# Low halves of one stage's weights prepared a stage earlier, and a rotation moved from GpSimd to VectorE

## The chip, the cores and the metric

The kernel runs on 1 core of one Trainium2 chip. The metric is the device time of one execution in microseconds; lower is better. Engines are named as in the profile: PE (TensorE), PEld (its weight loads), DVE (VectorE), ACT (ScalarE), POOL (GpSimd) and SP (SyncE, which issues nearly all DMAs).

## What is computed

Two blocks of two layers each on a 256 x 1024 float32 activation. The part that matters here:

```python
x = sandwich(x, mod, g_pre, g_post, ffn)          # stages 1 and 3: SwiGLU, D_FF = 2816
...
def fox_s5_mixer(x, ...):                          # stage 4
    q, k, v, f_logit, u = split(x @ w_in)
    att = forgetting_attention(q, k, v, f_logit + f_bias)
    y = s5_scan(u, ...)                            # h_t = a h_(t-1) + b u_t, complex a
    y = gelu(y); y = y * sigmoid(y @ w_glu + b_glu)
    return concatenate([att, y]) @ w_out
```

The complex recurrence of `s5_scan` is computed in a frame that turns with the angle of `a`: the input is turned in with tables of cosines and sines, a real scan with the magnitude of `a` runs on the real and the imaginary part, and the result is turned out with the same tables.

## The kernel before

The network runs as eight stages in a row (`run`, L2234 on): hybrid mixer, FFN, dilated attention, FFN (stage 3), attention with state space (stage 4, `even`), mixture of experts, mLSTM, mixture of experts.

**Weights.** Every projection weight is cut into units of 128 x 1024 float32 (512 KB, counted as 0.524 MB here). A product is made of three float32r matmuls: high weight times high activation, low times high, high times low. So each unit needs a high half `whi` (the weight rounded to float32r) and a low half `wlo` (what the rounding left out). `raw` (L287) lets SP load a unit into one of six buffers `raw`; `prepare` (L317) then casts it on ACT into `whi` (L328) and subtracts on DVE into `wlo` (L329). For the first three units of a stage and those of two named weights the subtraction is POOL's (L325). `whi` and `wlo` have five buffers each; during an FFN its output weights use three more. `split` (L332) hands out the next unit in the fixed order of `plan_of` (L343) and keeps two more prepared ahead, also across the stage boundary: the last units of stage 3 prepare the first three of stage 4.

**Background work.** Each unit handed out counts one tick; every `EVERY[st]` ticks (L690) one step of a background generator runs (`tick`, `step`). In stage 3 the generator is `modulation(3)`: eight steps, each a 512 KB load and one DVE pass of 128 x 1024 (L719). `drain` runs what is left. Instructions inside `later()` are placed behind the last evacuations of the stage join on their engine.

**Stage 3** (`ffn`, L760 on) takes 66 units: four at the start, then 21 times two input units and one output unit, less the ends. Between them ACT and DVE make the hidden values (`fs` L768, `fh` L770, `fhh`, `fhl`), on which the next output product waits.

**Stage 4** (`even`, L1522 on) has 26 units: 4 `ev_u`, 4 `ev_v`, 8 `ev_qk`, 8 `ev_out`, 2 `s5_glu`. Its attention (`fox`) and its state space (`state_space`) alternate. `state_space(jj)` runs four times with four quarters each. A quarter: PE projects into `eb` (L1576); DVE turns in with two products from PSUM (L1580, L1581), an add and a subtract within SBUF (L1582, L1583), and two scans (L1587); POOL turns out with two products of 128 x 512 (`eoc` L1590, `eos` L1591). After four quarters PE sums them into `ey` (L1597) and DVE adds the skip term (L1599). The order of instructions on each engine, SP's queue included, is fixed when the program is built; each engine and queue works through its own in order and waits on semaphores.

Of the kernel before, what the change touches and what calls it, by code (L numbers as in the profile page):

```python
# [9 lines left out]
F32 = mybir.dt.float32  # L10
F32R = mybir.dt.float32r
# [4 lines left out]
ALU = mybir.AluOpType  # L16
# [11 lines left out]
UNIT = 1024  # L28
# [199 lines left out]
class K:  # L228
# [87 lines left out]
    def prepare(self):  # L316
        nc = self.nc  # L317
        name, i = self.plan.pop(0)
        r = self.raw(name, i)
        pool = self.xtra.get(name, self.spl)  # L320
        hi = pool.tile([128, UNIT], F32R, tag="whi", name=self.nm("whi"))
        lo = pool.tile([128, UNIT], F32R, tag="wlo", name=self.nm("wlo"))
        if (name, i) in self.early:
            nc.scalar.copy(hi, r)  # L324
            nc.gpsimd.tensor_tensor(lo, r, hi.bitcast(F32), op=ALU.subtract)  # L325
        else:
            with self.later():
                nc.scalar.copy(hi, r)  # L328
                nc.vector.tensor_tensor(lo, r, hi.bitcast(F32), op=ALU.subtract)  # L329
        self.ready.append(((name, i), hi, lo))  # L330

    def split(self, name, i):  # L332

# [353 lines left out]
                self.feat(act, t, x, None, None)  # L687
        return act

    EVERY = (0.9, 1.6, 1.5, 2.0)  # L690


    def mod_setup(self):
# [65 lines left out]
    def ffn(self, act, l, hook=None):  # L759
        nc = self.nc  # L760
        ps = [[self.pso("fo") for n in range(2)] for t in range(2)]
        with self.tc.tile_pool(name=f"ff{l}", bufs=2) as P, self.tc.tile_pool(name=f"fx{l}", bufs=3) as X:

            def hidden(p):
                hh = P.tile([128, 256], F32R, tag="fhh", name=self.nm("fhh"), bufs=self.HOLD + 1)
                hl = P.tile([128, 256], F32R, tag="fhl", name=self.nm("fhl"), bufs=self.HOLD + 1)
                s = P.tile([128, 256], F32, tag="fs", name=self.nm("fs"))
                nc.scalar.activation(s, p[:, 0:256], AF.Silu)  # L768
                h = P.tile([128, 256], F32, tag="fh", name=self.nm("fh"))
                nc.vector.tensor_tensor(h, s, p[:, 256:512], op=ALU.mult)  # L770
                self.split_act(hh, hl, h)
                return hh, hl

            self.xtra = {"ffn_out": X}

            pp = [self.psw("pt"), self.psw("pt")]
            self.proj_b(act, "ffn_in", l * 44, 4, pp, True)
            if hook is not None:
                with self.later():
                    hook(P)  # L780
            hs = [[P.tile([128, 256], F32R, tag=g, name=self.nm(g), bufs=self.HOLD + 1) for g in ("fhh", "fhl")]
                  for j in range(2)]
            for t in range(2):
                ts = slice(t * 128, t * 128 + 128)
                s = P.tile([128, 256], F32, tag="fs", name=self.nm("fs"))
                nc.scalar.activation(s, pp[t][:, 0:256], AF.Silu)
                h = P.tile([128, 256], F32, tag="fh", name=self.nm("fh"))
                nc.vector.tensor_tensor(h, s, pp[t][:, 256:512], op=ALU.mult)
                pt = self.psw("fT")
                for j in range(2):  # L790
                    o = pt[:, j * 128:j * 128 + 128]
                    nc.tensor.transpose(o, h[:, j * 128:j * 128 + 128], self.ident)
                    self.split_act(hs[j][0][:, ts], hs[j][1][:, ts], o)
            late = []
            for j in range(22):
                if 2 <= j:
                    hs.append(None)
                    p = self.proj_a2(act, "ffn_in", l * 44 + j * 2)
                    self.down(ps, hs[j - 1], "ffn_out", l * 22 + j - 1, False, False, late if j > 22 - self.HOLD else None)
                    hs[j] = hidden(p)  # L800
                elif j == 0:
                    self.down(ps, hs[0], "ffn_out", l * 22, True, False)
            self.down(ps, hs[21], "ffn_out", l * 22 + 21, False, True, late)
            self.run_late(late)
            self.xtra = {}
        return ps

# [713 lines left out]
    def even(self, act):  # L1521
        nc, tc, a = self.nc, self.tc, self.a  # L1522
        with tc.tile_pool(name="ev", bufs=1) as P:
# [36 lines left out]
            def state_space(jj):  # L1560

                bt = self.rawp.tile([128, 4, 2, 128], F32, tag="raw", name=self.nm("raw"))
                nc.sync.dma_start(out=bt.rearrange("p a b c -> p (a b c)"), in_=a["s5_b"][jj])
                tabs = []
                for i in range(2):
                    tb = self.rawp.tile([128, 2, 2, 256], F32, tag="raw", name=self.nm("raw"))
                    nc.sync.dma_start(out=tb.rearrange("p a b c -> p (a b c)"), in_=self.s5d[jj * 2 + i])
                    tabs.append(tb)
                outs = []
                for q in range(4):  # L1570
                    j = jj * 4 + q
                    cb = tabs[q // 2][:, q % 2, 0:1, :].to_broadcast([128, 2, 256])
                    sb = tabs[q // 2][:, q % 2, 1:2, :].to_broadcast([128, 2, 256])
                    pb = self.psw("eb")
                    for i in range(2):
                        nc.tensor.matmul(pb[:, i * 256:(i + 1) * 256], bt[:, q, i, :], uT[:, jj, :], start=True, stop=True)  # L1576
                    pbv = pb.rearrange("p (i t) -> p i t", i=2)
                    m = self.tmp.tile([128, 2, 2, 256], F32, tag="big", name=self.nm("em"), bufs=2)
                    m1, m2 = m[:, 0], m[:, 1]
                    nc.vector.tensor_tensor(m1, pbv, cb, op=ALU.mult)  # L1580
                    nc.vector.tensor_tensor(m2, pbv, sb, op=ALU.mult)  # L1581
                    nc.vector.tensor_tensor(m1[:, 0], m1[:, 0], m2[:, 1], op=ALU.add)  # L1582
                    nc.vector.tensor_tensor(m1[:, 1], m1[:, 1], m2[:, 0], op=ALU.subtract)  # L1583
                    h = P.tile([128, 2, 256], F32, tag="eh", name=self.nm("eh"), bufs=2)
                    mg = self.s5m[:, j:j + 1].to_broadcast([128, 256])
                    for i in range(2):
                        nc.vector.tensor_tensor_scan(h[:, i, :], mg, m1[:, i, :], 0.0, ALU.mult, ALU.add)  # L1587
                    oc = P.tile([128, 2, 256], F32, tag="eoc", name=self.nm("eoc"), bufs=4)
                    os_ = P.tile([128, 2, 256], F32, tag="eos", name=self.nm("eos"), bufs=4)
                    nc.gpsimd.tensor_tensor(oc, h, cb, op=ALU.mult)  # L1590
                    nc.gpsimd.tensor_tensor(os_, h, sb, op=ALU.mult)  # L1591
                    outs.append((j, oc, os_))
                py = self.psw("ey")
                terms = ((0, 0, 0), (0, 1, 2), (1, 0, 2), (1, 1, 1))
                for ti, (w, i, ci) in enumerate(terms):
                    for q, (j, oc, os_) in enumerate(outs):
                        nc.tensor.matmul(py[32 * q:32 * q + 32, 0:256], s5c[:, ci, j, :], (oc, os_)[w][:, i, :],  # L1597
                                         start=(ti == 0), stop=(ti == 3))
                nc.vector.scalar_tensor_tensor(yg[:, jj, :], uT[:, jj, :], dsk[:, jj:jj + 1], py[:, 0:256],  # L1599
                                               op0=ALU.mult, op1=ALU.add)  # L1600
# [637 lines left out]
    def run(self, lo=0, hi=8):  # L2238
        nc, tc = self.nc, self.tc
        act = None  # L2240
        self.plan = [u for st in range(lo, min(hi, 5)) for u in self.plan_of(st)]
        self.xtra = {}
        self.early = {u for st in range(lo, 7) for u in self.plan_of(st)[:self.EARLY]}
        self.early |= {(n, i) for n, d in self.POOLED for i in range(0, 44, d)}
        if lo == 6:
            self.plan = self.plan_of(6)
        self.hi = hi

        def hook(P):
            self.s5_tables(P)  # L2250
# [8 lines left out]
        for st in range(lo, hi):  # L2259
# [4 lines left out]
            if st < 4:  # L2264
# [3 lines left out]
                if act is None:  # L2268
                    act = self.first_half()
                self.every = self.EVERY[st]  # L2270
                if st == 0:
                    ps = self.hybrid(act)
                elif st == 2:
                    ps = self.dilated(act)
                else:
                    ps = self.ffn(act, st // 2, hook if st == 1 else None)
                self.drain()
                act = self.join(ps, st, st < 3 and st + 1 < hi)
            else:
                if act is None:  # L2280
                    act = self.raw_logits((st - 5) // 2) if st % 2 else self.raw_feat()
# [39 lines left out]
```

## Time and profile before

| | us |
|---|---|
| median of 3 runs | 1425.95 (1425.86 to 1429.27) |
| the profiled execution's own time | 1426.13 |
| its span, first to last instruction | 1424.4 |
| PE busy / DVE busy / ACT busy / POOL busy | 1288.0 / 925.5 / 586.5 / 392.9 |

The profiled execution lies 0.18 us above the median, and 1.7 us of its time lie outside the span. Busy times are sums over the whole span; the stages differ, so what a change in one of them is worth is read from that stage: stage 3 runs from about 609 to 801 us, stage 4 from about 811 to 958 us. A DMA share is the mean busy share of the core's 16 DMA engines.

### The profile page before, as it was taken

To read this page: it belongs to the slowest core of one execution; us is meant where nothing else is said; L and a number is where in the kernel's file an instruction comes from. 1 tells how busy PE (TensorE), PEld (TensorE's weight loads), DVE (VectorE), ACT (ScalarE), POOL (GpSimd) and SP (SyncE) were. 2 spreads that over 40 slices of the span, in tenths; PEclk is the share of its full clock that TensorE was granted. 3 is DMA by queue.
4 is the path that set the end of the run, shared out by engine and by line. 5 is a ranking of instruction groups with operands and counts; after the bars stand their busy time and mean duration, and the time that the engine had idled before them with its cause. 6 is when DMAs were issued, how large, how long until landed. Compare 5 with 4: busy or idle time off the path is not lost. (4 is left out here: it accounts for less than half of the span.)

```text
span 1424.4 us, 21469 instructions
## 1 busy us (share of the span) xinstructions
PE 1288.0 (90%) x7869; PEld 1022.2 (72%) x7869; DVE 925.5 (65%) x1777; ACT 586.5 (41%) x986; POOL 392.9 (28%) x504
## 2 busy tenths in 40 slices
PE   5879779999977999999999988897999899989995
PEld 3757658999966999789999775675455599964442
DVE  6687978886557887586555678867222578764224
ACT  2443436444423564454444333353122467732122
POOL 2350443999993000200000424512000200020000
PEclk9989989999997999999999999998999999989998
DMA  8662746987617976277555453258987484469892
GB/s 305 238 222 109 275 148 235 348 293 244 212 70 283 337 223 208 90 261 256 189 181 179 151 192 119 89 207 325 400 320 303 153 324 166 147 223 356 316 375 92
DMA packets 97597, 326.31 MB, mean 229 GB/s; under 512 B 12512, under 2 KB 16304, under 8 KB 97480
## 3 DMA queue, kind: packets, MB, share of 16 engines
q1 hardware_dynamic: 96328, 320.62, 62.4%
q0 software_dynamic: 1152, 4.19, 0.8%
q8 instruction: 66, 1.08, 0.3%
q14 instruction: 51, 0.42, 0.1%
HBM read 319.49 MB, written 5.28 MB: 228 GB/s over the span
## 5 line engine op out<-in xcount | busy, mean ns | idle before, releaser
L329 DVE TENSOR_TENSOR wlo<-raw,whi 128x1024 fp32r<-128x1024 f32 x228 | 285.8, 1262 | 118.0 <-ACT whi L328 117.1
L328 ACT CAST whi<-raw 128x1024 fp32r<-128x1024 f32 x228 | 237.1, 1048 | 194.3 <-PE pa L425 84.9
L325 POOL TENSOR_TENSOR wlo<-raw,whi 128x1024 fp32r<-128x1024 f32 x34 | 84.2, 2491 | 495.0 <-ACT whi L324 426.3
L424 PE MATMUL pa<-hTh,whi 128*128 128x256 f32 x640 | 181.5, 284 | 0.0
L425 PE MATMUL pa<-hTl,whi 128*128 128x256 f32 x640 | 181.2, 283 | 0.0
L426 PE MATMUL pa<-hTh,wlo 128*128 128x256 f32 x640 | 181.0, 283 | 0.0
L425 PEld LDWEIGHTS pa<-hTl,whi 128*128 128x128 f32 x640 | 122.7, 192 | 1.9 <-issue 0.2
L424 PEld LDWEIGHTS pa<-hTh,whi 128*128 128x128 f32 x640 | 122.6, 192 | 2.1 <-issue 0.2
L426 PEld LDWEIGHTS pa<-hTh,wlo 128*128 128x128 f32 x640 | 122.8, 192 | 0.2
L1900 PE MATMUL mg<-mw,xT 128*64 128x512 f32 (+1 forms) x576 | 112.9, 545 | 0.0
L719 DVE SCALAR_TENSOR_TENSOR modp<-raw,cs,modp 128x1024 f32<-128x1024 f32 x70 | 98.7, 1410 | 4.9 <-DMA raw<-in_ada_w 3.3
L1900 PEld LDWEIGHTS mg<-mw,xT 128*64 128x64 f32 x576 | 41.0, 137 | 67.7 <-issue 61.0
L821 PE MATMUL fo<-whi,fhh 128*128 128x512 f32 x176 | 69.8, 399 | 1.9 <-ACT fhh L365 1.8
L822 PE MATMUL fo<-wlo,fhh 128*128 128x512 f32 x176 | 69.8, 396 | 0.0
L2063 DVE TENSOR_TENSOR hd<-hs,mg 128x128 f32<-128x128 f32 x33 | 9.5, 287 | 88.4 <-ACT hs L2061 88.4
L2076 DVE SCALAR_TENSOR_TENSOR yl<-my,cw,yh 128x512 fp32r<-128x512 f32 x34 | 25.5, 751 | 54.6 <-ACT yh L2075 53.8
L2169 PE MATMUL my<-mw,hT 128*64 128x512 f32 x256 | 58.5, 598 | 2.1 <-ACT hT L2067 2.1
L424 PE MATMUL aqk<-hTh,whi 128*128 128x256 f32 x192 | 55.8, 291 | 0.0
L825 PE MATMUL fo<-whi,fhl 128*128 128x512 f32 x176 | 55.4, 396 | 0.0
L426 PE MATMUL aqk<-hTh,wlo 128*128 128x256 f32 x192 | 54.9, 286 | 0.0
L425 PE MATMUL aqk<-hTl,whi 128*128 128x256 f32 x192 | 54.6, 285 | 0.0
L2061 ACT ACTIVATE hs<-mg 128x128 f32<-128x128 f32 x33 | 9.2, 277 | 110.0 <-PE mg L1900 100.9
(640 smaller groups left out, 3325.6 us busy)
## 6 DMA issues: line engine op xcount, KB each, us to landing
mw<-in_moe_w SPq DMA_DIRECT2D x204, 512.0 KB
raw<-in_ada_w SPq DMA_DIRECT2D x96, 512.0 KB
raw<-in_ffn_in SPq DMA_DIRECT2D x88, 512.0 KB
raw<-in_ffn_out SPq DMA_DIRECT2D x44, 512.0 KB
raw<-in_att_qk SPq DMA_DIRECT2D x24, 512.0 KB
raw<-in_od_qk SPq DMA_DIRECT2D x16, 512.0 KB
raw<-in_att_v SPq DMA_DIRECT2D x12, 512.0 KB
raw<-in_hyb_fq SPq DMA_DIRECT2D x8, 512.0 KB
```

Of the source, the lines that this page charges most:

```text
L325: nc.gpsimd.tensor_tensor(lo, r, hi.bitcast(F32), op=ALU.subtract)
L328: nc.scalar.copy(hi, r)
L329: nc.vector.tensor_tensor(lo, r, hi.bitcast(F32), op=ALU.subtract)
L424: nc.tensor.matmul(o, wh[:, c], hi[:, k, :], start=(k == 0), stop=False)
L425: nc.tensor.matmul(o, wh[:, c], lo[:, k, :], start=False, stop=False)
L426: nc.tensor.matmul(o, wl[:, c], hi[:, k, :], start=False, stop=(k == 7))
L719: V.scalar_tensor_tensor(acc, w, self.cs[:, k:k + 1], acc, op0=ALU.mult, op1=ALU.add)
L821: nc.tensor.matmul(ps[t][n], hh[:, ts], wh[:, c], start=first, stop=False)
L822: nc.tensor.matmul(ps[t][n], hh[:, ts], wl[:, c], start=False, stop=False)
L825: self.summed = nc.tensor.matmul(ps[t][n], hl[:, ts], wh[:, c], start=False, stop=last)
L1900: self.nc.tensor.matmul(G[64 * h:64 * h + 64, :], xT[:, k, s0 + 64 * h:s0 + 64 * h + 64], w[h][:, k2 * 512 + c0:k2 * 512 + c1], start=(k = ...
L2169: nc.tensor.matmul(y[n][64 * h:64 * h + 64, :], hT[f][:, 64 * h:64 * h + 64], ws[f][h][:, n * 512:(n + 1) * 512], start=(f == 0), stop=(f ...
```

## The change

Two things are changed. First, `lows_ahead` is a new background generator of stage 3, queued behind `modulation(3)`. For each of the 26 units of stage 4 it loads the unit into `raw`, casts it on ACT, subtracts on DVE, and has SP store the low half into a DRAM tensor `lowd`. In stage 4 `prepare` loads the low half from `lowd` straight into `wlo` with a second DMA in place of the subtraction; the cast on ACT stays and is no longer inside `later()`. `EVERY` of stage 3 goes from 2.0 to 1.8 ticks, and the background is drained before the stage's pools are closed. Second, the two products that turn the state out of its frame go from POOL to DVE.

```diff
@@ prepare
-        if (name, i) in self.early:
+        if (name, i) in self.lows:
+            nc.sync.dma_start(out=lo.bitcast(F32), in_=self.lowd[self.lows[name, i]])
+            nc.scalar.copy(hi, r)
+        elif (name, i) in self.early:
             nc.scalar.copy(hi, r)
             nc.gpsimd.tensor_tensor(lo, r, hi.bitcast(F32), op=ALU.subtract)
@@
+    def lows_ahead(self, P, st):
+
+        nc = self.nc
+        todo = self.plan_of(st)
+        self.lowd = self.dram.tile([len(todo), 128, UNIT], F32, name="lowd")
+        for n, (name, i) in enumerate(todo):
+            r = self.raw(name, i)
+            hi = P.tile([128, UNIT], F32R, tag="ahi", name=self.nm("ahi"), bufs=1)
+            lo = P.tile([128, UNIT], F32R, tag="alo", name=self.nm("alo"), bufs=2)
+            nc.scalar.copy(hi, r)
+            nc.vector.tensor_tensor(lo, r, hi.bitcast(F32), op=ALU.subtract)
+            nc.sync.dma_start(out=self.lowd[n], in_=lo.bitcast(F32))
+            self.lows[name, i] = n
+            yield
@@
-    EVERY = (0.9, 1.6, 1.5, 2.0)
+    EVERY = (0.9, 1.6, 1.5, 1.8)
@@ ffn
             self.run_late(late)
+            self.drain()
             self.xtra = {}
@@ even, state_space
-                    nc.gpsimd.tensor_tensor(oc, h, cb, op=ALU.mult)
-                    nc.gpsimd.tensor_tensor(os_, h, sb, op=ALU.mult)
+                    nc.vector.tensor_tensor(oc, h, cb, op=ALU.mult)
+                    nc.vector.tensor_tensor(os_, h, sb, op=ALU.mult)
@@ run
+        self.lows = {}
...
+        def hook2(P):
+            self.bg.append(self.lows_ahead(P, 4))
...
-                    ps = self.ffn(act, st // 2, hook if st == 1 else None)
+                    ps = self.ffn(act, st // 2, hook if st == 1 else hook2 if hi > 4 else None)
```

## Rows read from the trace of the kernel before

**Rows 1.** Windows: stage 3, then three stretches of stage 4.
```profile
core 0: us, PE busy (x) PEld busy (x) DVE busy (x) ACT busy (x) POOL busy (x), PEclk, DMA share, GB/s
623.00:801.00 178.00, 177.60 (x1231) 165.58 (x1232) 103.11 (x126) 79.07 (x112) 7.20 (x3) 1.00 0.59 207
811.00:835.00 24.00, 23.89 (x159) 21.49 (x160) 13.03 (x21) 11.57 (x17) 1.98 (x3) 0.96 0.82 288
835.00:931.00 96.00, 77.75 (x480) 53.82 (x478) 84.34 (x163) 32.39 (x76) 47.39 (x32) 0.97 0.30 103
931.00:958.00 27.00, 25.74 (x137) 21.20 (x137) 14.30 (x34) 17.17 (x34) 0.55 (x2) 0.97 0.64 223
```

**Rows 2.** Waits, 801 to 960 us: waiter <- releaser: us in total, times, longest.
```profile
PEld ey L1597 <- POOL eoc L1590: 20.5, 15, 2.7
DVE euT L1599 <- PE ey L1597: 6.5, 4, 3.5
```

**Rows 3.** Cast and subtraction of a unit in stage 3: ns minimum/median/maximum, first and last start.
```profile
L328 ACT CAST whi<-raw x63: 1038/1047/1058, 614.3 to 781.4; 128x1024 fp32r<-128x1024 f32 x63
...
L329 DVE TENSOR_TENSOR wlo<-raw,whi x59: 1204/1226/1227, 622.1 to 782.5; 128x1024 fp32r<-128x1024 f32 x59
```

**Rows 4.** Timeline of SP's queue in stage 3: start us, us, what was issued.
```profile
667.34 0.33 SPq L290 DMA_DIRECT2D raw<-in_ffn_out  x1
...
675.90 0.33 SPq L290 DMA_DIRECT2D raw<-in_ffn_out  x1
```

**Rows 5.** Windows of 10 us early in stage 3, columns as in rows 1.
```profile
621.00:631.00 10.00, 9.35 (x59) 7.81 (x58) 9.97 (x14) 6.12 (x10) 0.00 (x0) 1.00 0.98 368
631.00:641.00 10.00, 10.00 (x74) 9.49 (x74) 9.57 (x10) 4.68 (x6) 0.00 (x0) 1.00 0.97 350
641.00:651.00 10.00, 10.00 (x69) 9.27 (x68) 8.44 (x10) 6.30 (x9) 0.00 (x0) 1.00 0.98 363
```

**Rows 6.** A window of 10 us of stage 1, the first FFN.
```profile
266.00:276.00 10.00, 10.00 (x75) 9.49 (x74) 9.94 (x12) 3.85 (x5) 10.00 (x5) 1.00 1.00 348
```

**Rows 7.** A window of 10 us of stage 5, the mixture of experts.
```profile
1055.00:1065.00 10.00, 10.00 (x48) 3.55 (x45) 1.79 (x3) 1.65 (x3) 0.00 (x0) 1.00 1.03 411
```

**Rows 8.** Windows of the low halves alone: PE, PEld, DVE, POOL busy; clock; DMA.
```profile
835.00:931.00 96.00, 21.89 (x72) 13.99 (x72) 15.91 (x9) 0.00 (x0) 0.97 0.30 103
```

**Rows 9.** Groups by line, DVE, 801 to 958 us: busy us, mean ns | idle.
```profile
L1582 DVE TENSOR_TENSOR em<-em 128x256 f32<-128x256 f32 x16 | 14.4, 900 | 0.0
...
L1583 DVE TENSOR_TENSOR em<-em 128x256 f32<-128x256 f32 x16 | 9.8, 610 | 0.0
```

**Rows 10.** One line's instructions: ns minimum/median/maximum.
```profile
L1582 DVE TENSOR_TENSOR em<-em x16: 404/734/1523, 837.3 to 921.7; 128x256 f32<-128x256 f32 x16
```

**Rows 11.** Timeline of DVE, two products of 128 x 512 in a row.
```profile
839.13 0.66 DVE L1580 TENSOR_TENSOR em<-eb,raw 128x512 f32<-128x512 f32 x1
839.72 0.67 DVE L1581 TENSOR_TENSOR em<-eb,raw 128x512 f32<-128x512 f32 x1
```

**Rows 12.** Timeline of DVE, end of the last state-space group.
```profile
923.43 1.26 DVE L1587 TENSOR_TENSOR_SCAN eh<-s5mag,em 128x256 f32<-128x256 f32 x2
924.61 5.59 DVE L329 TENSOR_TENSOR wlo<-raw,whi 128x1024 fp32r<-128x1024 f32 x3
931.13 0.48 DVE L1599 SCALAR_TENSOR_TENSOR euT<-euT,edsk,ey 128x256 f32<-128x256 f32 x1 [0.93 <-PE ey L1597]
```

**Rows 13.** Timeline of POOL, the same stretch.
```profile
924.83 2.10 POOL L1590 TENSOR_TENSOR eoc<-eh,raw 128x512 f32<-128x512 f32 x1 [1.94 <-DVE eh L1587]
926.89 2.24 POOL L1591 TENSOR_TENSOR eos<-eh,raw 128x512 f32<-128x512 f32 x1
```

**Rows 14.** Waits of SP's own queue, whole span: us in total, times, longest.
```profile
SPq L290 <- DVE wlo L329: 285.4, 151, 7.5
```

**Rows 15.** DMA issues: KB each, median us from issue to landing.
```profile
s5tab<-s5E POOLq DMA_DIRECT2D x8, 512.0 KB, 4.2
```

## The prediction

> **What bounds the kernel now.** First the windows by stage [rows 1]. In stage 3 PE is busy 177.6 of 178 us while DVE is at 58% and ACT at 44%: PE sets the pace and nothing there can be gained, only lost. The DMA engines carry 207 GB/s at a share of 0.59, so there is room, but not without end. In stage 4 the picture changes twice. From 811 to 835 us PE has 23.9 of 24 us. From 835 to 931 us, the four state-space groups with attention between them, DVE is busy 84.3 of 96 us and PE 77.8: DVE is the bound, with POOL at 47.4. After 931 us PE is the busiest again, 25.7 of 27.
>
> Second, the waits of stage 4 [rows 2]: PE's weight loads for `ey` wait 20.5 us on POOL's `eoc`, and the skip term on DVE waits 6.5 us on `ey`. So POOL's two products sit at the end of a chain that starts on DVE.
>
> Third, what DVE does between 835 and 931 us. Nine subtractions into `wlo` take 15.9 us [rows 8], 1.77 us each, where one takes 1.226 us in stage 3 [rows 3]. The add and the subtract of 128 x 256 take 900 and 610 ns on average [rows 9], but the shortest of them 404 and the longest 1523 ns [rows 10]. The long ones fall where POOL works: DVE and POOL hold each other up when both read SBUF.
>
> **The change, part by part.**
>
> *Low halves in stage 3.* A step adds one ACT cast (1.05 us), one DVE subtraction (1.23 us) [rows 3], two SP issues (0.33 us each [rows 4]) and two DMAs of 0.524 MB. There are 8 + 26 = 34 steps; at 1.8 ticks they need 61 of the 66 ticks, so they end inside the stage and before the first unit of stage 4 is prepared. DVE goes from 103 to 103 + 26 x 1.23 = 135 of 178 us, ACT from 79 to 106. PE hides both: in stage 1 PE stays at 10.00 of 10 us with DVE at 9.94 [rows 6]. If that cover went, each step would cost up to 2.3 us.
>
> The DMAs are the serious term. Three units take 675.90 - 667.34 = 8.56 us [rows 4], 2.85 us each. The 26 steps run over 45 ticks = 128 us, in which 45 FFN loads, 26 loads and 26 stores are due: 97 x 0.524 = 50.9 MB, 397 GB/s. With the DMA engines full, this stage has moved 368, 350 and 363 GB/s [rows 5], mean 360, and stage 1 348 [rows 6]; the mixture of experts reaches 411 [rows 7]. At 360 the 50.9 MB take 141 us, 13 too many, of which the six `raw` buffers loaded ahead cover 6 x 0.524/0.360 = 8.7: +4 us. At 411 it is nothing; at 348, 146 - 128 - 9 = +9. A gain is excluded, since PE is full. I take +4, from this stage's own rows; ends 0 and +9. The stores are the unknown in it: the only row of a 512 KB store shows 4.2 us to landing [rows 15] and nothing against them moving at the loads' rate.
>
> The Trainium skill, HBM Reference, section Specifications (TRN2), gives a core about 358 GB/s as its share of the memory and about 425 when it streams alone. By the first this term would be +5, by the second 0; rows 5 look like the first, rows 7 like the second.
>
> *Stage 4, DVE.* Removed between 835 and 931 us: nine subtractions, 15.9 us [rows 8]. Removed with POOL's work: the hold-ups, 14.4 - 16 x 0.404 = 7.9 us on the add and 9.8 - 16 x 0.405 = 3.3 on the subtract [rows 9, 10], 11.2 together. Added: 32 products of 128 x 512. The trace has none with both inputs in SBUF; 256 columns take 0.40 and 1024 take 1.23 us, which gives 0.68, and two neighbours of that size from PSUM take 0.66 and start 0.59 us apart [rows 11]. So 32 x 0.59 = 18.9 us. Balance -15.9 - 11.2 + 18.9 = -8.2 us on the engine that sets the pace.
>
> *Stage 4, the end of the chain.* After the last scan, at 924.7 us, POOL works until 929.1 and the skip term starts at 931.1 [rows 12, 13]: 6.4 us. With DVE doing both products at once it is 2 x 0.59 + the same 2.0 = 3.2, so -3. Earlier groups end the same way, but there DVE has the next group's work to do, so I count one end only. Stage 4 in all: -11. It can't gain more than 96 - 77.8 = 18, when PE takes over as the bound. At the other end, if the hold-ups don't go, DVE has 18.9 - 15.9 = +3 more.
>
> *Stage 4, the other stretches.* The other fourteen subtractions on DVE, before 835 us and after 931, lie beside a full PE, as do POOL's three: nothing. What takes their place is 26 more loads. At 360 GB/s one is 1.46 us of all DMA engines. From 811 to 835 us the share is 0.82: 4.3 us are free, and about five of the low halves fall due there (7.3 us; the first ones can land before the join), so 0 to +3. From 931 us ten low halves (14.6 us) meet 27 x 0.36 = 9.7 us free and a long stretch before at 0.30: 0 to +2. I take +1 for both. The low loads wait on SP for PE to free `wlo`, with the table loads of the state space behind them; those are due a group later and are covered. The cast that leaves `later()` can stand before ACT's work in the join for one cast, 1 us at most, which is in that +1. The drain moved by a few lines issues the same instructions: nothing.
>
> *Sum*, against the profiled execution's 1426.1 (0.2 above the median): +4 - 11 + 1 = -6, 1420 us. The measurement tells changes of over 0.3%, 4.3 us, from none.
>
> **Rivals.**
>
> *No change (1426).* DVE's relief is real but the FFN gives it back: +9 in stage 3 at the rate of rows 6, -11 in stage 4, +3 from the loads: +1, 1427. For it: the demand of 397 GB/s is above every window of an FFN. Against: the ring of six. Generators that don't finish, so that nothing changes in stage 4, would end here too; the 61 of 66 ticks speak against it.
>
> *Slower: the stores hold SP's queue (about 1446).* In stage 3 a store waits on SP for its own load, cast and subtraction, and the loads for the FFN stand behind it. If SP stops for all of that, a step takes 4.2 (landing, as in rows 15) + 1.05 + 1.23 + 3.8 x 0.33 for issues = 7.7 us against 5.1 us of PE work in 1.8 ticks: 26 x 2.6 = +68, less 9 for the ring. At half of it, +30 with -11 and +1, 1446. Against: SP already waits for a subtraction before most loads, 151 times [rows 14], as a load needs the buffer that the subtraction frees; a store that waits for a subtraction in the same order holds nothing that wasn't held. It decides from 0.7 us of added hold per step: 26 x 0.7 = 18, which undoes ring and gain.
>
> *Slower: DVE is full and just gets more (1434).* If the long adds have another cause than POOL, stage 4 is +3, and with +4 and +1 the time is 1434. For it: 88% busy. Against: minimum and maximum of the same instruction [rows 10] and POOL's times.
>
> The Trainium skill, Perfetto Trace Analysis, section Optimizing Scalar/DVE Operations, speaks against this move: from a saturated DVE work may go to GpSimd, not the other way. It adds that the two share a read port, so that such moves might not help; the rows so far are for that second half.
>
> **How the numbers follow.** Forecast 0.56, no change 0.20, SP's queue 0.13, DVE full 0.11. The forecast's own range is 1408 (0 - 18 + 0) to 1421.8, where no change begins. The range of 8 in 10 adds no change and DVE full and stops short of most of the SP case: 1408 to 1435. Faster 0.56, same 0.20, slower 0.24.
>
> **What would show it.** In the changed profile: stage 3 from 623 us on with PE near full, a DMA share near 1.0 over some 130 us, and not over 182 us long for the same PE work; casts waiting on DMA there, by a few us in sum. Between the start and the end of the state space: some 85 us in place of 96, the adds at 0.41 us, 32 DVE products at 0.6 to 0.7, no POOL. It would be wrong if stage 3 had PE idle behind loads for over 10 us, if the products took over 1 us, or if stage 4's first matmuls waited for low halves from DRAM.

## The result, and the profile after

| | before | changed |
|---|---|---|
| median, us | 1426.50 (13 runs, 1422.96 to 1429.36) | 1434.99 (13 runs, 1430.27 to 1439.45) |
| the profiled execution's own time / span, us | 1426.13 / 1424.4 | 1439.45 / 1437.2 |

The ratio is 1.0061, 95% interval 1.0048 to 1.0074: the change costs some 9 us where 6 were to be gained. It is slower by more than the 0.3% that the prediction named, and 1435 lies at the range's upper end. The profiled execution of the changed kernel is the slowest of its 13, 4.5 us above their median. In the changed kernel the cast and the subtraction of `prepare` stand 3 lines further down (L331, L332); the lines of the stages stand 18 or 19 further down, so that the `fo` of L821 is that of L840.

Three starts in the rows of tiles place the loss: stage 3's first `fo`, stage 4's first `eu`, stage 5's first `mg`. In the kernel before (engine, tiles, times: ns minimum/median/maximum, first to last start in us):

```profile
L821 PE MATMUL fo<-whi,fhh x88: 389/393/502, 623.3 to 800.2; 128*128 128x512 f32 x88
L825 PE MATMUL fo<-whi,fhl x88: 388/390/477, 624.4 to 800.8; 128*128 128x512 f32 x88
...
L424 PE MATMUL eu<-hTh,whi x32: 280/283/562, 810.1 to 823.1; 128*128 128x256 f32 x32
...
L1900 PE MATMUL mg<-mw,xT x332: 379/592/643, 984.4 to 1299.9; 128*64 128x512 f32 x134, 128*64 128x256 f32 x32
```

In the changed kernel:

```profile
L840 PE MATMUL fo<-whi,fhh x88: 387/394/504, 626.5 to 816.0; 128*128 128x512 f32 x88
L844 PE MATMUL fo<-whi,fhl x88: 387/391/632, 627.5 to 816.7; 128*128 128x512 f32 x88
...
L442 PE MATMUL eu<-hTh,whi x32: 278/283/364, 824.6 to 836.6; 128*128 128x256 f32 x32
...
L1919 PE MATMUL mg<-mw,xT x298: 379/592/643, 997.5 to 1299.9; 128*64 128x512 f32 x117, 128*64 128x256 f32 x32
```

The first `fo` came 3.2 us later, ahead of the first low half (its load is issued at 642.8 us); in the runs below that start lies anywhere from 619.9 to 626.5, so it is left out. **Stage 3**, first `fo` to first `eu`, took 198.1 us where it took 186.8: +11.3, for the +4 of the prediction. **Stage 4**, first `eu` to first `mg`, took 172.9 for 174.3: -1.4, for the -10. From `mg` on nothing changed.

The windows of the changed kernel, columns as in [rows 1]: stage 3 in two parts, then the first state-space group and the stretch behind it.

```profile
626.00:731.00 105.00, 104.54 (x731) 97.74 (x732) 76.81 (x87) 59.07 (x78) 0.00 (x0) 1.00 0.90 327
731.00:801.00 70.00, 61.99 (x419) 55.67 (x418) 42.56 (x46) 36.78 (x45) 0.00 (x0) 1.00 0.90 327
...
845.00:866.00 21.00, 20.37 (x126) 15.57 (x125) 18.63 (x36) 4.31 (x5) 0.00 (x0) 1.00 1.03 409
866.00:882.00 16.00, 11.90 (x41) 7.26 (x41) 2.89 (x18) 8.41 (x23) 0.00 (x0) 0.68 0.43 161
```

For 105 us of stage 3 PE stays full, as in [rows 1]; then 8 of 70 us are lost. (The prediction had named PE idle behind loads for over 10 us as a sign of being wrong, and the whole stage lost 11.3.) In both parts the DMA engines carry 327 GB/s at a share of 0.90: they are not full although work for them is late. What holds it back stands in SP's own waits in stage 3, 623 to 812 us:

```profile
SPq L346 <- DVE alo L345: 98.6, 25, 7.0
SPq L290 <- DVE wlo L332: 11.5, 10, 2.4
```

Before, SP waited in this stage for `wlo` above all, that is for a buffer; [rows 14] is for the whole span, and this row is of stage 3, 623 to 801 us:

```profile
SPq L290 <- DVE wlo L329: 84.3, 41, 3.5
```

Now it stands 98.6 us, 25 times, at the stores, each waiting for its own subtraction. What comes late for it, among ACT's waits of the same stretch:

```profile
ACT whi L331 <- DMA raw<-in_ffn_in: 19.0, 20, 4.6
...
ACT whi L331 <- DMA raw<-in_ffn_out: 14.0, 16, 4.1
```

The casts of the FFN's own weights wait for loads that SP issued late, and PE's weight loads wait for those casts and their subtractions. In the kernel before the same two casts waited 2.8 us in sum. ACT before, and PEld in the changed kernel:

```profile
ACT whi L328 <- DMA raw<-in_ffn_in: 2.3, 3, 1.3
...
ACT whi L328 <- DMA raw<-in_ffn_out: 0.5, 1, 0.5
```

```profile
PEld fo L840 <- ACT whi L331: 5.1, 3, 2.5
PEld pa L444 <- DVE wlo L332: 4.1, 6, 1.0
```

In stage 4 the parts moved as foretold. The wait of `ey` [rows 2] and the adds and subtracts [rows 9], with the products on DVE:

```profile
PEld ey L1616 <- DVE eoc L1609: 2.7, 5, 1.6
```

```profile
L1609 DVE TENSOR_TENSOR eoc<-eh,raw 128x512 f32<-128x512 f32 x16 | 10.9, 680 | 0.0
L1610 DVE TENSOR_TENSOR eos<-eh,raw 128x512 f32<-128x512 f32 x16 | 10.9, 680 | 0.0
L1602 DVE TENSOR_TENSOR em<-em 128x256 f32<-128x256 f32 x16 | 6.6, 415 | 0.0
L1601 DVE TENSOR_TENSOR em<-em 128x256 f32<-128x256 f32 x16 | 6.6, 414 | 0.1
```

20.5 us of waiting on POOL became 2.7 on DVE, and 24.2 us of adds and subtracts became 13.2. The gain went into a hole: from 866 to 882 us DVE works 2.89 of 16 us (windows above), and PE 11.90, at a granted clock of 0.68, a mean between its two levels of 1.2 and 2.4 GHz. The timeline of DVE there, cut to the hole's two ends:

```profile
865.47 0.48 DVE L1618 SCALAR_TENSOR_TENSOR euT<-euT,edsk,ey 128x256 f32<-128x256 f32 x1 [1.96 <-PE ey L1616]
...
881.58 0.42 DVE L1668 TENSOR_TENSOR yl<-eo,yh 128x256 fp32r<-128x256 f32 x1 [5.83 <-ACT yh L1667]
881.92 0.68 DVE L1599 TENSOR_TENSOR em<-eb,raw 128x512 f32<-128x512 f32 x1
```

and of PE and of SP's queue:

```profile
866.38 0.43 PE L1640 MATMUL es<-enc,e 40*128 40x384 f32 x1
...
875.53 1.11 PE L1665 MATMUL eo<-ept,ev__8678 128*64 128x256 f32 x2
878.02 0.63 PE L1659 MATMUL ept<-cm,esc 128*128 128x128 f32 x2
878.66 1.05 PE L1595 MATMUL eb<-euT,raw 128*128 128x256 f32 x2
...
881.07 3.29 PE L1595 MATMUL eb<-euT,raw 128*128 128x256 f32 x14
```

```profile
844.84 4.39 SPq L1938 DMA_DIRECT2D mw<-in_moe_w  x6
...
855.35 0.33 SPq L1582 DMA_DIRECT2D raw<-in_s_b  x1
856.63 1.61 SPq L1586 DMA_DIRECT2D raw<-s5tab  x2
```

Before, the second group's `eb` stood among the `es` of the first attention block in PE's order; now they stand behind its `eo`, so DVE has no state-space work while that block runs. In SP's order low loads and six loads for the mixture of experts (`mw`, `moe_ahead`) now stand back to back ahead of that group's tables, which are issued only at 855 to 858 us.

### The profile page after: what moved, and what is told of

The parts are those of the page before. It is cut to its first block, busy times and chain, and to the rows that moved or that the text cites. A ratio compares the mean times of both kernels' runs of the same rounds, so it can differ in the third digit from the quotient of the medians.

```text
span 1437.2 us, 21564 instructions
## 1 busy us (share of the span) xinstructions
PE 1299.9 (90%) x7869; PEld 1027.8 (72%) x7869; DVE 929.6 (65%) x1812; ACT 613.5 (43%) x1012; POOL 337.8 (24%) x469
## 5 line engine op out<-in xcount | busy, mean ns | idle before, releaser
L332 DVE TENSOR_TENSOR wlo<-raw,whi 128x1024 fp32r<-128x1024 f32 x205 | 256.1, 1257 | 83.4 <-ACT whi L331 82.2
L331 ACT CAST whi<-raw 128x1024 fp32r<-128x1024 f32 x205 | 212.9, 1048 | 144.7 <-PE pa L443 34.7
L328 POOL TENSOR_TENSOR wlo<-raw,whi 128x1024 fp32r<-128x1024 f32 x31 | 77.8, 2523 | 319.1 <-ACT whi L327 314.1
L840 PE MATMUL fo<-whi,fhh 128*128 128x512 f32 x176 | 67.6, 399 | 6.3 <-ACT whi L331 4.5
```

Source lines behind the costliest of these rows:

```text
L840: nc.tensor.matmul(ps[t][n], hh[:, ts], wh[:, c], start=first, stop=False)
```

## The experiments

Three spans are read from the tile rows as above: *fo*, first to last `fo` of stage 3; *stage 3*, first `fo` to first `eu`; *stage 4*, first `eu` to first `mg`. Ratios are to the kernel before, with the 95% interval; a span from one profile also moves between kernels that have the same work in it: stage 4 by up to 2.5 us (e1 and e5 to e7), and a stage 3 that loses time by up to 5.6 (the changed kernel, e2 and e4: 198.1, 194.1, 199.7). So the loss of stage 3 is 7 to 13 us, and where two kernels lose there, differences smaller than this spread say nothing.

| kernel | fo | stage 3 | stage 4 | ratio |
|---|---|---|---|---|
| before | 177.5 | 186.8 | 174.3 | 1 |
| changed | 190.2 | 198.1 | 172.9 | 1.0061 (1.0048 to 1.0074) |
| e1 turn only | 177.4 | 186.4 | 173.5 | 0.9974 (0.9957 to 0.9991) |
| e2 lows only | 186.2 | 194.1 | 179.0 | 1.0094 (1.0066 to 1.0123) |
| e3 stores on POOL's queue | 188.4 | 198.3 | 165.7 | 1.0004 (0.9979 to 1.0029) |
| e4 `mw` loads later | 191.7 | 199.7 | 167.5 | 0.9999 (0.9977 to 1.0020) |
| e5 no store | 177.2 | 186.1 | 171.0 | 0.9959 (0.9941 to 0.9978) |
| e6 stores only | 177.1 | 186.0 | 171.2 | 0.9958 (0.9940 to 0.9976) |
| e7 casts, subtractions only | 177.2 | 186.0 | 171.4 | 0.9948 (0.9927 to 0.9969) |
| e8 ten units | 181.8 | 191.1 | 166.3 | 0.9932 (0.9907 to 0.9957) |
| e9 ten units, spread | 177.2 | 186.2 | 167.1 | 0.9945 (0.9931 to 0.9959) |
| e10 loads, stores apart | 179.0 | 191.3 | 166.8 | 0.9986 (0.9970 to 1.0001) |
| e11 half stores | 177.8 | 187.0 | 172.7 | 0.9985 (0.9971 to 0.9998) |
| e12 load ahead | 190.2 | 197.4 | 173.2 | 1.0072 (1.0049 to 1.0096) |
| e13 store later | 187.5 | 195.9 | 171.9 | 1.0057 (1.0036 to 1.0078) |
| e14 both shifts, `mw` later | 179.3 | 188.1 | 162.8 | 0.9940 (0.9919 to 0.9960) |
| e15 POOL's queue, load ahead | 186.1 | 196.1 | 164.5 | 0.9980 (0.9963 to 0.9998) |
| e16 both shifts alone | 179.2 | 188.0 | 169.7 | 0.9989 (0.9974 to 1.0004) |

**The parts (e1, e2).**

```diff
 e1: before, with
-nc.gpsimd.tensor_tensor(oc, h, cb, op=ALU.mult)
-nc.gpsimd.tensor_tensor(os_, h, sb, op=ALU.mult)
+nc.vector.tensor_tensor(oc, h, cb, op=ALU.mult)
+nc.vector.tensor_tensor(os_, h, sb, op=ALU.mult)
 e2: changed, with these two lines the other way round
```

> The kernel before with only the turn out of the frame on DVE, no low halves made ahead. Markers in the kernel before: stage 4's first eu matmul 810.0 us, stage 5's first mg matmul 984.4. By the prediction's own terms the move alone costs 18.9 us of products on DVE, gives back 11.2 of hold-ups and 3 at the end of the chain: stage 4 is 5 us longer (mg about 989) and the time 1431. Rival: the 20.5 us that PE waited on POOL's products were the true bound; then the stage is shorter, mg at 975 to 980 and the time 1417 to 1422. Either way stage 3 is untouched, eu at 810 within 2 us, and the adds take 0.41 us.

> The changed kernel with the turn out of the frame back on POOL. Stage 3 must stay as in the changed kernel: first eu about 824, 14 us late. In stage 4 the nine subtractions are gone but POOL's hold-ups are back, and the order of PE's matmuls still has the second group's eb behind the first attention block. If that order eats the gain, stage 4 takes as long as before or longer (mg minus eu 173 to 180 us) and the time is 1437 to 1444; if the move of the products is what eats it, stage 4 is 164 to 168 us and the time is about 1430.

The turn alone gains 0.26%: better than the 5 us lost by the prediction's terms, less than the rival's 5 to 10 gained. (Its first `eu` stood at 806.4, not within 2 us of 810; its first `fo` was 3.3 us early already.) DVE's groups between 806 and 980 us show a term that the expectation left out:

```profile
L329 DVE TENSOR_TENSOR wlo<-raw,whi 128x1024 fp32r<-128x1024 f32 x23 | 27.9, 1215 | 10.3 <-ACT whi L328 10.3
```

The subtractions take 1215 ns with POOL silent; the nine among the state-space groups took 1770 before [rows 8], so POOL held these up too. The prediction had read that and removed these subtractions whole; where they stay, as in e1, 9 x 0.55 = 5.0 us come back, as much as was to be lost. The low halves alone make the kernel slower. In e2 PE waits on POOL again:

```profile
PEld ey L1616 <- POOL eoc L1609: 22.7, 16, 1.8
```

So the turn is a gain alone, and beside the low halves stage 4's span says the same (179.0 against 172.9), though the two ratios' intervals overlap there; the loss is the low halves'. Stage 3 of e2, which was to stay as in the changed kernel with `eu` at about 824, came out 4 us shorter with `eu` at 815.3: the spread named above.

**Which part of a step costs stage 3 (e5, e6, e7).** All three with the turn on DVE and stage 4's weights split there as before.

```diff
 e5:
-            nc.sync.dma_start(out=self.lowd[n], in_=lo.bitcast(F32))
-            self.lows[name, i] = n
 e6: all seven lines of the step's body become
+            nc.sync.dma_start(out=self.lowd[n], in_=r)
 e7: as e5, and without
-            r = self.raw(name, i)
 e6, e7: r is one tile, set once ahead of the loop
```

> Stage 3 as in the changed kernel but without the stores: 26 times a load, a cast and a subtraction whose result is used by nobody; stage 4 subtracts as before, with its turn on DVE. The stretch from the first to the last fo matmul of stage 3 was 177.5 us before and 190.2 in the changed kernel. The bytes due over 45 ticks (128 us) fall from 50.9 to 37.2 MB, 290 GB/s. If it is the sum of bytes that can't be served (some 325 GB/s were), the stretch falls to 177 to 181. If stores only add bytes like any other and the loads, the casts and the raw buffers are the cost, it stays at 184 to 190.

> Stage 3 with 26 stores of 512 KB from one tile that stays as it is, no load, no cast and no subtraction beside them; stage 4 as in the kernel with the turn alone. Again 290 GB/s. If only the sum of bytes counts, the stretch of fo matmuls is 177 to 181 us, as without the stores. If a store costs the DMA engines more than a load of the same size, it is longer than that kernel's by several us, 183 to 190.

> Stage 3 with the 26 casts and 26 subtractions alone, made of one tile that stays in SBUF: no DMA is added. If PE hides ACT's 27 us and DVE's 32 us, as the prediction had it, the stretch of fo matmuls is 177 to 179 us. If the work of the engines in front of the hidden values and of the FFN's own casts is part of the loss, it is 181 to 188.

None of the three costs anything: loads with engine work, stores by themselves and engine work by itself are all hidden. PE hides 26 casts and subtractions, as the prediction had it, and neither 26 loads nor 26 stores show a price by themselves (four of the stores in e6 were issued at 611 us, ahead of the first `fo`). That left the sum of bytes, or something that only whole steps have.

**Bytes or waits (e3, e10, e11).**

```diff
 e3: changed, with
-            nc.sync.dma_start(out=self.lowd[n], in_=lo.bitcast(F32))
+            nc.gpsimd.dma_start(out=self.lowd[n], in_=lo.bitcast(F32))
 e10: e5, and in each step a store of one tile z, set once
+            nc.sync.dma_start(out=self.lowd[n], in_=z)
 e11: e5, and in each step half a store
+            nc.sync.dma_start(out=self.lowd[n][:, 0:512], in_=lo.bitcast(F32)[:, 0:512])
```

> The changed kernel with its 26 stores issued from POOL's queue, so that none stands in SP's queue ahead of a load. If SP's queue held by stores that wait for a subtraction made stage 3 longer, its loads come early again: eu back at 810 to 813 and the time at 1421 to 1424. If the DMA engines can't serve 397 GB/s, it makes no difference: eu at 821 to 826, waits on the FFN's raw loads as before, time 1432 to 1437.

> Stage 3 with the 26 loads, casts and subtractions and with 26 stores beside them, but each store sends a tile that stays in SBUF and waits for no subtraction. The bytes are those of the changed kernel: 50.9 MB in 128 us, 397 GB/s; stage 4 as with the turn alone. If bytes are the cause, the stretch of fo matmuls is 186 to 191 us, as in the changed kernel. If it is the store that waits in SP's queue for its own subtraction, with loads behind it, the stretch is 177 to 181, since loads alone and stores alone cost nothing.

> The 26 steps whole, each store waiting for its subtraction, but only half of each low half is stored: 44.0 MB due in 128 us, 344 GB/s; stage 4 as with the turn alone. If bytes are the cause, the stretch of fo matmuls lies between 177 (at 290 GB/s) and 190 (at 397): 181 to 186. If the waiting stores are the cause, their size changes little: 187 to 190. If the limit is a rate of some 360 GB/s, as the prediction took it, 177 to 179.

e10 issues the bytes of the changed kernel, though four of its 26 stores already at 610 us, ahead of the first `fo`; it lost 4.5 us, not 11.3, and most of that (3 us) came behind the last `fo`. e11 keeps the waits (the rows below are SP's at its stores, 623 to 812 us) and lost 0.2.

```profile
SPq L346 <- DVE alo L345: 42.5, 14, 4.4
SPq L346 <- DVE fh L787: 32.6, 8, 5.2
SPq L346 <- DVE fhl L383: 17.8, 4, 5.3
```

By e10 the waits are the cause, by e11 the bytes count too, and a limit near 360 GB/s fits it: neither the bytes nor the waiting stores suffice alone. In e3 stage 3 kept its whole loss although no store stands in SP's queue, as if bytes were all; its time is lower than that theory had it because stage 4 came out without the hole. Windows of e3, then of e10, 665 to 735 and 735 to 805 us:

```profile
665.00:735.00 70.00, 65.25 (x451) 59.82 (x450) 46.65 (x50) 40.77 (x50) 7.44 (x14) 1.00 0.99 376
735.00:805.00 70.00, 67.93 (x469) 62.99 (x469) 40.94 (x46) 37.05 (x48) 4.79 (x9) 0.98 1.00 359
```

```profile
665.00:735.00 70.00, 70.00 (x498) 65.91 (x498) 45.58 (x50) 37.59 (x49) 0.00 (x0) 1.00 0.98 362
735.00:805.00 70.00, 68.73 (x465) 62.78 (x464) 45.85 (x52) 40.45 (x57) 8.53 (x5) 1.00 0.90 325
```

In e3 the DMA engines are full (0.99 and 1.00, for 0.90 in the changed kernel), and PE loses 4.75 us already ahead of 735. There it waits for the FFN's `fhh`. The `fs` that this is made from stands on ACT behind two casts for low halves that wait for their own loads (the timelines of ACT and of PE, e3):

```profile
715.78 1.05 ACT L344 CAST ahi<-raw 128x1024 fp32r<-128x1024 f32 x1 [4.12 <-DMA raw<-in_ev_qk]
...
719.09 1.05 ACT L344 CAST ahi<-raw 128x1024 fp32r<-128x1024 f32 x1 [1.32 <-DMA raw<-in_ev_qk]
720.05 0.38 ACT L786 ACTIVATE fs<-pa 128x256 f32<-128x256 f32 x1
...
721.76 0.41 ACT L383 CAST fhh<-fh 128x256 fp32r<-128x256 f32 x1 [0.41 <-DVE fh L788]
```

```profile
722.22 0.50 PE L840 MATMUL fo<-whi,fhh 128*128 128x512 f32 x1 [2.29 <-ACT fhh L383]
```

**Taking the waits away (e12 to e16).** A step lasts 1.8 ticks, 5.1 us of PE work. In the timelines of SP and ACT in the changed kernel a low half's cast starts 4.8 to 9.8 us after its load is issued, and cast and subtraction take 1.05 + 1.23 us more [rows 3]. A store right behind its load makes SP wait for all of that; one step between them should take off 5.1 us, two steps 10.2 us.

```diff
 e12 (load ahead):
+        nxt = self.raw(*todo[0])
         for n, (name, i) in enumerate(todo):
-            r = self.raw(name, i)
+            r, nxt = nxt, self.raw(*todo[n + 1]) if n + 1 < len(todo) else None
 e13 (store later; three buffers alo):
-            nc.sync.dma_start(out=self.lowd[n], in_=lo.bitcast(F32))
+            if old is not None:
+                nc.sync.dma_start(out=self.lowd[n - 1], in_=old.bitcast(F32))
+            old = lo
...
+        nc.sync.dma_start(out=self.lowd[len(todo) - 1], in_=old.bitcast(F32))
 e4: changed; e14: e12 and e13; both with
-            self.moe_ahead(0)
             for jj in range(1, 4):
                 fox(jj - 1, self.pso)
                 state_space(jj)
+                if jj == 2:
+                    self.moe_ahead(0)
 e15: e3 and e12    e16: e12 and e13
```

> The changed kernel with each low half's load issued one step ahead of its cast, so that the cast, which stands on ACT ahead of the FFN's own, finds its data there. From the first fo matmul of stage 3 to the first eu matmul it was 186.8 us before, 198.1 in the changed kernel, 191.3 with loads and stores that don't wait for each other. If the loss beyond bytes is the cast waiting for its load on ACT, and the subtraction and store behind it, this falls to 190 to 193. If it is the store waiting on SP for a subtraction that other work delays, it stays at 195 to 199.

> The changed kernel with each low half stored one step later, so that SP finds the subtraction done and no load stands behind it; the cast still follows its own load. If SP's queue held by the stores (98.6 us of waits in stage 3) is the loss beyond bytes, first fo to first eu falls from 198.1 to 190 to 193 us. If the casts that wait on ACT for their loads are, it stays at 195 to 199, as it did with the stores on POOL's queue (198.3).

> Load one step ahead and store one step later, and the six loads for the mixture of experts behind the third state-space group: the same bytes as in the changed kernel, with neither wait. If waits make all of the loss beyond bytes, first fo to first eu is 189 to 192 us, stage 4 165 to 169, and the time about 1424. If the bytes themselves make it, it is 196 to 199 and the time about 1430.

SP's waits at the stores, 623 to 812 us, in e12, in e13 (a second row is the last store's), in e14:

```profile
SPq L347 <- DVE alo L346: 80.9, 22, 6.2
```

```profile
SPq L348 <- DVE alo L346: 74.1, 20, 6.5
...
SPq L352 <- DVE alo L346: 6.7, 1, 6.7
```

```profile
SPq L349 <- DVE alo L347: 14.6, 9, 6.1
```

98.6 us in the changed kernel, 80.9 and 80.8 with one step between load and store, 14.6 with two. Waits at the same stores that are put down to another releaser (`fhl`, `fh`, `pa`) come on top; with them it is 101.6, 91.7, 95.2 and 21.9. The loss of stage 3 goes with it: 11.3, 10.6 and 9.1, which the spread above doesn't tell apart, and 1.3, which stands clear of them. e12 and e13 each missed what their own theory gave; what they share is the distance. With all bytes of the change, e14 loses 1.3 us in stage 3, and came out better than expected in all three: 0.9 us in stage 3, 2.2 in stage 4, and 1417.4 us of time where about 1424 was expected. Its windows there, 665 to 735 and 735 to 805 us, show PE near full:

```profile
665.00:735.00 70.00, 70.00 (x498) 65.92 (x498) 43.68 (x49) 35.50 (x48) 0.00 (x0) 1.00 0.94 340
735.00:805.00 70.00, 68.70 (x456) 62.19 (x456) 46.02 (x54) 41.56 (x59) 0.62 (x2) 1.00 0.92 349
```

> The 26 stores on POOL's queue and each load one step ahead of its cast. With the stores on POOL's queue alone, SP was free and the DMA engines full, and still first fo to first eu took 198.3 us: ACT stood 41 us at casts whose load had not landed. If that wait is the second half of the cause, taking it away as well gives 188 to 192 us, as with both shifts (188.1). If stores through POOL's queue are slower in themselves, it stays at 196 to 199.

> Both shifts, but the six loads for the mixture of experts where the changed kernel has them. If the two losses are separate, first fo to first eu is 187 to 190 us as with both shifts, stage 4 (first eu to first mg) is back at 171 to 174 with DVE idle for over 10 us in the first attention block, and the time is 1425 to 1429. If the shifts alone bring stage 4 its gain, it is 163 to 166 and the time 1417 to 1420.

e15 kept the loss (196.1), so the wait that e3 showed is not cured by a load one step ahead: the casts still waited 37.5 us for their loads in it (16.6 for those of `ev_out` alone) while the DMA engines moved 391 and then 346 GB/s. Why loads land later with the stores on a second queue stays open. e16 shows the two losses to be separate: stage 3 is healed as in e14, stage 4 is not (169.7 for 162.8, a little better than expected), and the time lies between.

**Stage 4's hole (e4).**

> The changed kernel with the six loads that run ahead for the mixture of experts placed behind the third state-space group instead of ahead of the second; nothing else moved by hand. In the order built from it, the eb matmuls of the second group stand among the es matmuls of the first attention block again. If the gap of 16 us on DVE at 866 to 882 is what ate the gain of stage 4, stage 4 (mg minus eu, 174.4 before and 172.9 in the changed kernel) falls to 161 to 166 us and the time to 1424 to 1428; stage 3 stays 14 us long. If the groups only slide and another limit holds them, stage 4 stays at 170 to 173 and the time at 1432 to 1436.

With the six loads moved, the `eb` of the second group stand among the `es` again and stage 4 falls to 167.5 us, 1.5 above what was expected; the time is in the expected range, that of the kernel before, as stage 3 keeps its loss. In e14, PE's timeline at the first attention block:

```profile
853.71 0.44 PE L1645 MATMUL es<-enc,e 40*128 40x384 f32 x1
854.08 1.13 PE L1600 MATMUL eb<-euT,raw 128*128 128x256 f32 x4
855.05 0.38 PE L1651 MATMUL es<-ekz,eq 128*128 128x128 f32 x2
```

By the ratios, too, the six loads cost their share: e4 lies 8.8 us under the changed kernel and e14 7.0 under e16, each pair apart by their place alone.

**Fewer units (e8, e9).** Only the units whose subtractions fall between the state-space groups.

```diff
-        todo = self.plan_of(st)
+        todo = [u for u in self.plan_of(st) if u in self.FEW]   # ev_qk 0 to 7, ev_out 0 and 1
 e8:
-    EVERY = (0.9, 1.6, 1.5, 1.8)
+    EVERY = (0.9, 1.6, 1.5, 3.4)
 e9: EVERY of stage 3 is 2.0, and lows_ahead begins with
+        self.every = 4.4
```

> The changed kernel with low halves made ahead for ten units only (the eight of ev_qk and the first two of ev_out, whose subtractions fall between the state-space groups), one step every 3.4 ticks. Per step 3.4 FFN loads, a load and a store are due in 9.7 us: 292 GB/s. If the demand for bytes is what stage 3 paid for, the stretch of fo matmuls is 178 to 181 us and stage 4 keeps the gain (mg minus eu 163 to 169 us): 1416 to 1421, below both kernels. If every step costs stage 3 its share whatever the rate (13 us over 26 steps, 0.5 us each), the stretch is 182 to 183 and the time 1421 to 1424.

> Ten low halves as in the kernel with ten, but the modulation keeps its step every 2.0 ticks and only the ten steps behind it are spread, one every 4.4 ticks: 6.4 units in 12.5 us, 268 GB/s. The 4.3 us that ten low halves cost stage 3 fell into one stretch, 685 to 695 us, where a cast for a low half waited 2.9 us for its load ahead of the FFN's own cast, at the end of the modulation. If that meeting was the loss, the stretch of fo matmuls is 177 to 179 us, stage 4 stays at 166 to 168, and the time is 1414 to 1419. If ten steps cost 4 us wherever they stand, it is 181 to 183 and the time about 1420.

Both beat both kernels. e8 lost 4.3 us of its *fo* span, most of it in one stretch, 685 to 695 us, while its median came out as low as expected; e9 lost nothing there. In e9 the three spans come as expected and the time 0.6 us above the expected range, at 1419.56. With its order left alone (`mw` loads as in the change), ten low halves don't open the hole. The best versions are e8, e9 and e14 (medians 1420.2, 1419.6 and 1417.4); their intervals overlap.

## Why the prediction was wrong

**The DMA term of stage 3 (+4, ends 0 and +9) was right as a price of bytes**: with the change's 50.9 MB e14 lost 1.3 us, and e10, four stores of it issued ahead, 4.5. The full DMA engines that it was worked out from (a share near 1.0 over some 130 us) did not come: e14 shows 0.94 and 0.92. The rate was no fixed one: 327 GB/s in the changed kernel at a share of 0.90, 340 to 349 in e14, 376 over 70 us in e3. The Trainium skill, HBM Reference, section Specifications (TRN2), has about 358 GB/s as a core's share and about 425 alone; the stretches of 376 and 391 lie between, so the first was no ceiling here.

**The step that failed in stage 3 is the argument against the rival of SP's queue**: that SP "already waits for a subtraction before most loads", so that a store that waits "in the same order holds nothing that wasn't held". The 151 waits [rows 14] are those of the whole span; stage 3 had 41. They are for a buffer that a subtraction some loads back frees; a store waits for the subtraction of the load just ahead of it, and meanwhile nothing new is issued. It also showed in the profile as that rival had it: 98.6 us of waits, 3.8 per step, far above the 0.7 from which it was said to decide. Only its price was off, +68 less the ring or half of it (+30): the held time replaced most of the old waits for `wlo` (84.3 us before, 11.5 now), and by e14 and the change it cost 10.0 us (198.1 - 188.1). By the ratios it is 8.4 us: e14 differs from e4 by the two shifts alone. Part of that price can be the low halves' casts that wait on ACT for their loads (17.2 us in the changed kernel, 0.5 in e14), as both shifts take these away too. That a held SP queue is not the only way to lose it is shown by e3, where those casts waited 41.0 us with no store in SP's queue. The Trainium skill, DMA: Bandwidth & Descriptors, section Anatomy of one DMA — SWDGE (gpsimd) path, says that DMA engines wait on no semaphore and the issuing sequencer does; the rows of SP agree.

**The terms of stage 4 were right in kind, the order was not.** Adds at 0.41 us, products at 0.68 that start 0.59 apart, `ey` freed of POOL: all as foretold. In e14, where the order is whole, stage 4 is 174.3 - 162.8 = 11.5 us shorter, for -11 + 1. That this sum fits so well is in part luck: from the first `eb` to the last skip term it is 88.6 us for 96.9 before, -8.3 of the -11, and the rest came outside that stretch, where +1 was forecast. The step that failed is the one that put the table loads behind the low loads and called them "due a group later and ... covered". Their data did land in time: no `eb` of the changed kernel waits for a load, and in e14 and e16 these tables are issued equally late, 9.5 us behind the first group's first `eb`, with the hole in e16 alone. But the order of PE, fixed when the program is built, had moved the second group's `eb` behind the attention block, and that cost 172.9 - 162.8 = 10.1 us by the spans, 7 to 9 by the ratios. That the order hangs on where those DMAs stand is shown by e4 and e16 against e14. It is not enough that the six loads stand ahead of the tables: they do so too in the kernel before and in e3, which have no hole, but there they are spread, from 802.6 to 824.4 us and from 814.2 to 842.3. How the builder weighs them was not looked into.

**The rivals.** Not DVE: the number of that rival (1434) came true, its mechanism did not, since DVE was idle 13 of 16 us in the hole and its adds were short. The Trainium skill, Perfetto Trace Analysis, section Optimizing Scalar/DVE Operations, speaks of moves off a saturated DVE and adds that moves between DVE and GpSimd might not help, as the two share an SBUF read port. Here e1 moved work onto DVE and gained 0.26%, with the subtractions at 1215 ns for 1770; that fits the shared port, and no rule against such a move. The forecast's sum, -6 us, lies at the near end of what the change gives once both orders are mended: e14 is 8.6 us faster by its ratio (5.7 to 11.6).

## What to carry to other kernels

A DMA that waits for a result holds its queue: place it behind its own load by more than the time from load to result, here two background steps of 5.1 us for some 9, or the loads behind it are issued late although the sum of bytes looks affordable. When a change adds DMAs to a kernel whose order is fixed at build time, compare the new order of every engine with the old one around the bound stage before counting a saving; seven to ten us went here where no term of the sum looked. And make only as much ahead as the bound stretch asks for: ten of 26 units brought most of the gain for two fifths of the traffic.

## What was not expected of the hardware

The prediction had read that POOL's two-input products slow DVE's adds and subtractions; not expected was that this makes the move pay by itself. With the subtractions at 1.22 for 1.77 us and the adds at 0.41, moving 32 products of 0.68 us onto a DVE that was 88% busy cost nothing (e1). Loads and stores mixed reached 376 and 391 GB/s over 70 us with the stores on POOL's queue, more than the loads alone early in stage 3 [rows 5], and stage 3 still lost 11.5 and 9.3 us: a fuller DMA share was no sign of less waiting.
